# A quarter of the MLP's weight halves take their low part from an accumulating DMA

## The chip, the cores and the metric

The kernel runs on one core of a Trainium2 chip. The metric is the device time of one execution in microseconds (us), the median over runs. The kernel before took 2235.47 and 2235.57 us in its two runs, a median of 2235.52 us.

The engines are called as the profile calls them: PE (TensorE, the matrix products), PEld (its weight loads), DVE (VectorE), ACT (ScalarE), POOL (GpSimd) and SP (SyncE, which here issues the loads from HBM).

## The reference

Two layers of a decoder trunk for 256 tokens of width 2048, all float32. Each layer adds a mixing sub-layer (attention heads and state-space heads beside each other) and an MLP. Only the MLP is touched by the change:

```
D_MODEL = 2048; SEQ = 256; DEPTH = 2; D_FF = 4 * D_MODEL
h = rmsnorm(x, ln2_g)
x = x + jnp.square(jax.nn.relu(h @ w_mlp_in)) @ w_mlp_out
```

`w_mlp_in` is 2048 x 8192 and `w_mlp_out` 8192 x 2048 in each layer, 64 MB each in float32.

## The kernel before, in words

**Split products.** The products run on float32r operands. To keep the accuracy, every float32 operand is split into a high part `hi` (the value rounded to float32r) and a low part `lo` (the value minus `hi`), and a product is the sum of three: hi*hi, hi*lo and lo*hi. Activations are split once and kept; weights are split as they arrive.

**Panels, halves and steps.** All weights come in panels of 128 partitions x 2048 float32 (1 MB, one DMA on SP's queue, tile `raw`, three buffers). A step is half a panel (128 x 1024): its split and the products that it goes into. The split is one ACT copy with a cast (`hi`, line 121) and one DVE subtraction (`lo` = raw - hi, line 126). `hi` and `lo` have five buffers each (LA + 1, with LA = 4).

**Order of the program.** The kernel builds one long list of steps, 754 in all, and then writes the instructions out step by step; nothing reorders them afterwards. At step i the loop first writes the split of step i + 4 (`convert`), then the load of the panel two further on (`load_to`), then the products of step i, then, where a step ends a group, its `post`. Each engine takes its own instructions in this order and waits by semaphores. The five buffers mean that the split of step i + 4 writes the buffers that step i - 1 has read, so it starts when the products of step i - 1 are done, about when those of step i begin.

**The MLP.** It goes by eight groups of 1024 hidden columns in each layer. `mlp1` of a group has 16 steps: weights stationary (`w_units`, lines 215 to 219), eight pairs of matmuls per step, one on `hi` with 512 moving columns (activations' high and low parts side by side) and one on `lo` with 256. Every fourth step or so ends a unit of 256 hidden columns, and its post adds the two halves (ACT copy line 425, DVE lines 426 and 822) and splits the result (ACT line 121, DVE line 126 on 128 x 256). `mlp2` of a group has 16 steps too: activations stationary (`x_group`, lines 291 to 293), twelve matmuls of 512 columns per step, one third of them on `lo`; its post is two DVE instructions (line 833). The order is mlp1(0), mlp1(1), mlp2(0), mlp1(2), mlp2(1) and so on. In all there are 256 MLP steps in each layer, numbers 121 to 376 in the first and 498 to 753 in the second.

**POOL** does small elementwise work outside the MLP (and the power function of the norms, line 353); it issues no DMA before the change.

Of the kernel before, what the change touches and what calls it, by code (L numbers as in the profile page):

```python
# [31 lines left out]

# Columns of the shape-only constants.
K_ID, K_TRI, K_DIST, K_LNC, K_SEL, K_END = 0, 128, 256, 640, 1024, 1040
# Columns of the packed parameters, channels on the partitions.
V_G1, V_G2, V_GA, V_GS, V_DS, V_CW, V_CB, V_AL, V_DB, V_END = 0, 32, 64, 80, 96, 112, 208, 232, 264, 296
# [17 lines left out]
class Step:  # L54
    """Half a weight panel: its split into two float32r parts, and the products it goes into."""

    def __init__(self, panel, half, mm, post=None):
        self.panel, self.half, self.mm, self.post = panel, half, mm, post


class Panel:
    def __init__(self, src, shape):
        self.src, self.shape = src, shape
        self.raw = None
# [3 lines left out]
def trunk_kernel(ctx: ExitStack, tc, x_in, xT_in, w_in, w_v, w_dt, w_out, w1, w2, final_g, par_in, cst_in, out):  # L68
# [48 lines left out]
    def split(*parts):  # L117
        """hi + lo = src * g, each part of twelve significant bits."""
        for hi, lo, src, g in parts:
            if g is None:  # L120
                nc.scalar.copy(hi, src)  # L121
            else:
                nc.scalar.activation(hi, src, AF.Copy, scale=g)
        for hi, lo, src, g in parts:
            if g is None:
                nc.vector.tensor_tensor(lo, src, hi.bitcast(F32), op=ALU.subtract)  # L126
            else:
                nc.vector.scalar_tensor_tensor(lo, src, g, hi.bitcast(F32), op0=ALU.mult, op1=ALU.subtract)  # L128

    mm = nc.tensor.matmul  # L130

# [1 line left out]
    cst = const.tile([P, K_END], F32, name="cst")  # L133
# [51 lines left out]

# [1 line left out]
    tasks = []  # L187
# [14 lines left out]
    def stages(*fs, delay=1):  # L202
        """The first after this step or a later one, each other one a step later."""
        def g():
            for f in fs:
                f()
                yield 1
        spawn(g(), delay)

    steps = []  # L210

# [1 line left out]
    def whole_and_low(ps, wh, wl, r, k):  # L213
# [7 lines left out]
    def w_units(units, hT):  # L221
        """Weights stationary: out[col, token | its low part's products]. Two units at a time share
        the order of k so that the later half of the activations may come late."""
        def unit_steps(u):
            st = {}
            panels = [Panel(u["src"](kh), [P, 8, T]) for kh in range(2)]

            def mk(kq):
                def f(hi, lo):
                    if kq == 0:  # L230
                        st["ps"] = [acc(), acc()]
                    hv = hi.rearrange("p (k c) -> p k c", k=4)
                    lv = lo.rearrange("p (k c) -> p k c", k=4)
                    h = hT()
                    for ti in range(2):
                        ps = st["ps"][ti]
                        cs = slice(ti * P, (ti + 1) * P)
                        for kk in range(4):
                            k = kq * 4 + kk
                            r = h[k // 8][:, k % 8, :]  # L240
                            whole_and_low(ps, hv[:, kk, cs], lv[:, kk, cs], r, k)
                return f

            def post():
                for ti in range(2):
                    u["post"](ti, st["ps"][ti])

            return [Step(panels[kq // 2], kq % 2, mk(kq), post if kq == 3 else None) for kq in range(4)]

        for a in range(0, len(units), 2):  # L250
            ss = [unit_steps(u) for u in units[a:a + 2]]
            if a == 0 and len(ss) == 2:
                steps.extend(ss[0][:2] + ss[1][:2] + ss[0][2:] + ss[1][2:])
            else:
                for s in ss:
                    steps.extend(s)

    def x_group(src, nk, h_of, post, apart=False):
        """Activations stationary: out[token, 512 columns] over nk tiles of k. Apart: all of the first
        128 tokens before the second, and post by their halves."""  # L260
        st = {}
        panels = [Panel(src(i), [P, 4, 512]) for i in range(nk // 4)]

# [36 lines left out]
    def wide(w, l, r0, c0):  # L300
        """The panel of 512 rows and 512 columns from r0, c0."""
        return w[l, r0 // 512, c0 // 512]

    def tall(w, l, r0, c0):
        """The panel of 1024 rows and 256 columns from r0, c0."""
        return w[l, r0 // 1024, c0 // T]

# [1 line left out]
    def new_h():  # L309
# [5 lines left out]
    class Norm:  # L315
        """Sums of squares and split transposes of x, by its chunks of 512 columns."""

# [38 lines left out]
    def channel_rstd(ssq, n):  # L356
        """From squares with the channels on the partitions."""
        ps = sa()
        for t in range(2):
            mm(ps[:, t:t + 1], ssq[:, t * P:(t + 1) * P], ones[:, 0:1], start=True, stop=True)  # L360
        return finish_rstd(ps[:, 0:2], n)

    class FirstNorm:
        """The same from the transposed input, by its chunks of 512 channels."""

# [35 lines left out]

# [1 line left out]
    def layer(l, S, S_next):  # L403
        """S: this layer's state, with hT and norm of its first sub-layer; S_next: the next one's."""
        def rstdB_task():
# [14 lines left out]
        def joined(ps, n=P, scale=None):  # L420
            """The two halves of a weights-stationary product, summed."""
            p2 = p2p.tile([P, T], F32, tag="p2", name=nm("p2"))
# [8 lines left out]

        # x, B and C: convolution and SiLU, channels on the partitions.
        xs_t, bc_t = {}, {}
# [61 lines left out]

        # dt, the weights' two parts side by side: out[part and head, token | its low part's products].
        dts = {}
# [15 lines left out]
        steps.append(Step(Panel(w_dt[l], [P, 16, 16]), 0, dt_mm, dt_post))  # L513
        # v, tokens on the partitions.
        vt = {}
# [11 lines left out]

# [1 line left out]
        ssd = {}  # L529

        def ssd_prep():
            # dt = softplus(raw + bias), tokens on the partitions.
            ps = sa()
# [34 lines left out]
            yield 2  # L568
            # Running sums of dt * a in each chunk, and the decay to the first chunk's end.
            ps = sa()  # L570
# [48 lines left out]
        def ssd_group(g):  # L619
            """The group's inputs times dt, and its state after the first chunk."""  # L620
            xs, dt, dtd = xs_t["xs"], ssd["dt"], ssd["dtd"]
# [21 lines left out]
        def ssd_pair(j):  # L643
# [3 lines left out]
            for i in range(2):  # L647
                mm(ps[:, i * T:(i + 1) * T], sel[:, 2 * j + i:2 * j + i + 1].to_broadcast([32, P]), cumT,
                   start=True, stop=True)
            # Decays from s to t: where s is later than t, the exponent's bound keeps them finite and  # L650
            # cbs is zero.
            MT = ep.tile([P, 2, T], F32, tag="MT", name=nm("MT"))
# [47 lines left out]

# [1 line left out]
        att = {}  # L702
# [19 lines left out]
        def att_head(j, i):  # L722
            """Softmax of one head's scores; transposed, it is left in att["pt", h]."""
            q, k = att["qk", j, 0], att["qk", j, 1]
# [57 lines left out]

# [1 line left out]
        def out_post(c, which, ps):  # L784
# [28 lines left out]

# [1 line left out]
        acts = {}  # L815
# [10 lines left out]
        def mlp1(G):  # L826
            w_units([dict(src=lambda kh, u=u: tall(w1, l, kh * 1024, G * GF + u * T),
                          post=lambda ti, ps, u=u: mlp1_post(G, 2 * u + ti, ps)) for u in range(4)],
                    lambda: S["hT2"])
# [25 lines left out]
        def mlp2(G):  # L855
            for c in range(4):
                final = l == DEPTH - 1 and G == NG - 1 and c == 3
                x_group(lambda i, c=c: wide(w2, l, G * GF + i * 512, c * 512), 8,
                        lambda k: acts[G][:, k, :],
                        mlp2_last if final else lambda ps, c=c: mlp2_post(G, c, ps), apart=final)  # L860

# [6 lines left out]
    class Final:  # L868
        """The last norm and the output."""

# [46 lines left out]

# [1 line left out]
    panels = []  # L919
    for s in steps:  # L920
        if not panels or panels[-1] is not s.panel:
            if s.panel not in panels[-4:]:
                panels.append(s.panel)
    index = {id(p): i for i, p in enumerate(panels)}
    loaded = [0]

# [22 lines left out]
    def convert(s):  # L949
# [8 lines left out]
        else:  # L958
            split((s.hi, s.lo, src, None))

# [83 lines left out]
```

## Time and profile before

| | |
|---|---|
| median of two runs | 2235.52 us |
| span of the profiled execution, first to last instruction | 2233.3 us |
| PE busy | 2208.7 us, 99% of the span |
| DVE busy | 1460.3 us, 65% |
| ACT busy | 1058.4 us, 47% |
| POOL busy | 150.6 us, 7% |
| DMA engines, mean share (SP's queue) | 52.1% |

The profiled execution has its span alone on record; the runs' times lie 2.2 us above that span, which is taken as what lies around it. The row "mean share" of the DMA engines counts the time that packets took on the core's 16 DMA engines. PE's matmuls are pipelined: a matmul of 512 columns is shown with 0.39 us, but the next one starts 0.23 us after it, so the pace of PE is read from the distances between starts.

### The profile page before, as it was taken

The numbers are of one execution on the slowest core, as the hardware profiler recorded it, in microseconds if no ns is written. First come the engines' busy times: TensorE is split into PE (matmuls) and PEld (weight loads), VectorE is DVE, ScalarE is ACT, GpSimd is POOL, SyncE is SP. The second block draws the span as 40 slices with busy tenths as digits, with TensorE's granted clock in tenths as the row PEclk, the third lists the DMA queues.
The fourth block names the chain that finished last, engine by engine and source line by source line (L and its number), as shares of the span: only waits on it lengthen the run. The fifth ranks groups of instructions, "written<-read, shape, count | busy, mean of one in ns | idle before, by whom it ended". The sixth has DMA issues, their size and how long they took to land.

```text
span 2233.3 us, 29120 instructions
## 1 busy us (share of the span) xinstructions
PE 2208.7 (99%) x11444; PEld 1850.0 (83%) x11444; DVE 1460.3 (65%) x1997; ACT 1058.4 (47%) x1539; POOL 150.6 (7%) x201
## 2 busy tenths in 40 slices
PE   8999999999999999999999999999999999999998
PEld 6877778888888888888888777788888888888886
DVE  7757986665665655656666578866656656656565
ACT  6544554543444444434555455555444434444443
POOL 3102310000000000000011032100000000000001
PEclk9999999999999999999999999999999999999999
DMA  8454344555555555555554543455555555555554
GB/s 295 172 188 145 121 151 170 188 188 190 189 189 189 189 188 192 186 196 190 180 188 168 174 150 124 145 186 184 185 190 195 189 189 189 188 191 187 188 193 147
DMA packets 58249, 404.44 MB, mean 181 GB/s; under 512 B 6400, under 2 KB 6784, under 8 KB 10240
## 3 DMA queue, kind: packets, MB, share of 16 engines
q1 hardware_dynamic: 58112, 402.58, 52.1%
q8 instruction: 90, 1.47, 0.3%
q14 instruction: 47, 0.39, 0.0%
HBM read 400.45 MB, written 2.10 MB: 180 GB/s over the span
## 4 chain that ended last, share of the span: by engine, by line
PE 95%; DVE 3%; issue 1%; ACT 0%; DMA 0%; POOL 0%; SPq 0%; ACTq 0%; POOLq 0%; DVEq 0%
PE acc L215 30%; PE acc L216 15%; PE acc L291 14%; PE acc L293 14%; PE acc L292 14%; PE acc L219 2%; PE acc L218 1%; DVE lo L126 1%; PE sb L729 1%; PE sb L728 1%; DMA raw<-in_w_in 0%; PE sb L748 0%; PE sb L765 0%; PE acc L505 0%; DVE h L128 0%
## 5 line engine op out<-in xcount | busy, mean ns | idle before, releaser
L126 DVE TENSOR_TENSOR lo<-raw,hi 128x1024 fp32r<-128x1024 f32 x752 | 921.5, 1235 | 613.4 <-ACT hi L121 613.1
L121 ACT CAST hi<-raw 128x1024 fp32r<-128x1024 f32 x754 | 783.3, 1048 | 718.6 <-PE acc L293 414.2
L215 PE MATMUL acc<-h,hi 128*128 128x512 f32 x3000 | 1077.0, 401 | 8.7 <-DVE h L128 8.7
L216 PE MATMUL acc<-h,lo 128*128 128x256 f32 x3000 | 843.4, 281 | 2.2 <-DVE lo L126 2.2
L215 PEld LDWEIGHTS acc<-h,hi 128*128 128x128 f32 x3000 | 565.3, 188 | 147.1 <-issue 10.2
L216 PEld LDWEIGHTS acc<-h,lo 128*128 128x128 f32 x3000 | 568.3, 189 | 11.4 <-DVE lo L126 2.5
L291 PE MATMUL acc<-hi,m 128*128 128x512 f32 x1280 | 501.0, 391 | 0.0
L293 PE MATMUL acc<-hi,m 128*128 128x512 f32 x1280 | 498.3, 389 | 0.0
L292 PE MATMUL acc<-lo,m 128*128 128x512 f32 x1280 | 498.1, 389 | 0.0
L291 PEld LDWEIGHTS acc<-hi,m 128*128 128x128 f32 x1280 | 240.3, 188 | 51.5 <-issue 3.0
L293 PEld LDWEIGHTS acc<-hi,m 128*128 128x128 f32 x1280 | 240.3, 188 | 50.2
L292 PEld LDWEIGHTS acc<-lo,m 128*128 128x128 f32 x1280 | 240.4, 188 | 49.2
L121 ACT CAST m<-a 128x256 fp32r<-128x256 f32 x128 | 52.1, 407 | 153.6 <-DVE a L822 153.6
L425 ACT COPY p<-acc 128x256 f32<-128x256 f32 x186 | 68.9, 370 | 66.6 <-PE acc L219 61.4
L126 DVE TENSOR_TENSOR m<-a,m 128x256 fp32r<-128x256 f32 x128 | 54.4, 425 | 60.5 <-ACT m L121 60.5
L833 DVE SCALAR_TENSOR_TENSOR x_sb<-acc,r,x_sb 128x512 f32<-128x512 f32 x128 | 89.9, 743 | 4.9 <-PE acc L293 4.9
L426 DVE TENSOR_TENSOR u<-acc,p 128x256 f32<-128x256 f32 x186 | 77.2, 417 | 17.1 <-ACT p L425 17.0
L219 PE MATMUL acc<-h,hi 128*128 128x512 f32 x200 | 80.0, 400 | 0.0
L353 POOL TENSOR_TENSOR rstd<-ms,nhalf 128x2 f32<-128x2 f32 x10 | 8.8, 882 | 873.9 <-DVE ms L351 862.7
L822 DVE SCALAR_TENSOR_TENSOR a<-u 128x256 f32<-128x256 f32 x128 | 54.4, 425 | 4.4
L218 PE MATMUL acc<-h,lo 128*128 128x256 f32 x200 | 56.6, 283 | 0.0
L886 POOL TENSOR_TENSOR x_sb<-x_sb,final_g 128x512 f32<-128x512 f32 x6 | 8.6, 1454 | 687.3 <-DMA final_g<-in_final_norm_g 672.1
(167 smaller groups left out, 1169.7 us busy)
## 6 DMA issues: line engine op xcount, KB each, us to landing
raw<-in_w_mlp_in SPq DMA_DIRECT2D x128, 1024.0 KB, 4.9
raw<-in_w_mlp_out SPq DMA_DIRECT2D x128, 1024.0 KB, 4.9
raw<-in_w_in SPq DMA_DIRECT2D x69, 1024.0 KB, 4.9
raw<-in_w_out SPq DMA_DIRECT2D x32, 1024.0 KB, 4.8
raw<-in_w_v SPq DMA_DIRECT2D x16, 1024.0 KB, 4.9
raw<-in_w_in SPq DMA_DIRECT2D x6, 512.0 KB, 9.0
xT<-in_xT SPq DMA_DIRECT2D x4, 512.0 KB, 8.6
x_sb<-in_x SPq DMA_DIRECT2D x4, 512.0 KB, 6.5
```

The costliest lines, as they stand in the source:

```text
L121: nc.scalar.copy(hi, src)
L126: nc.vector.tensor_tensor(lo, src, hi.bitcast(F32), op=ALU.subtract)
L215: mm(ps, wh, r, start=(k == 0), stop=False)
L216: mm(ps[:, 0:T], wl, r[:, 0:T], start=False, stop=False)
L218: mm(ps[:, 0:T], wl, r[:, 0:T], start=False, stop=False)
L219: mm(ps, wh, r, start=False, stop=True)
L291: mm(ps, ah, hv[:, kk, :], start=(k == 0), stop=False)
L292: mm(ps, ah, lv[:, kk, :], start=False, stop=False)
L293: mm(ps, al, hv[:, kk, :], start=False, stop=(k == nk - 1))
L425: nc.scalar.copy(p2[:n], ps[:n, T:2 * T])
L426: nc.vector.tensor_tensor(u[:n], ps[:n, 0:T], p2[:n], op=ALU.add)
L833: nc.vector.scalar_tensor_tensor(xc, ps[t], S["r2"][:, t:t + 1], xc, op0=ALU.mult, op1=ALU.add)
```

## The change

Steps whose number in the list is 3 modulo 4 and whose panel belongs to the MLP (marked `far`) get `lo` in another way. ACT writes `hi` as before, then writes -hi into `lo` (the same read of `raw`, scale -1.0, rounded the same way), and then a DMA issued by POOL reads the same half panel from HBM a second time and adds it onto `lo`. There are 128 such steps, 64 in each layer. The DVE subtraction of these steps is gone. The comments that the diff also removes are not shown.

```diff
 class Panel:
-    def __init__(self, src, shape):
-        self.src, self.shape = src, shape
+    def __init__(self, src, shape, far=False):
+        self.src, self.shape, self.far = src, shape, far
...
-            panels = [Panel(u["src"](kh), [P, 8, T]) for kh in range(2)]
+            panels = [Panel(u["src"](kh), [P, 8, T], u.get("far", False)) for kh in range(2)]
...
-    def x_group(src, nk, h_of, post, apart=False):
+    def x_group(src, nk, h_of, post, apart=False, far=False):
...
-        panels = [Panel(src(i), [P, 4, 512]) for i in range(nk // 4)]
+        panels = [Panel(src(i), [P, 4, 512], far) for i in range(nk // 4)]
...
+    for i, s in enumerate(steps):
+        s.index = i
...
-            split((s.hi, s.lo, src, None))
+            far = s.panel.far
+            if far and s.index % 4 == 3:
+
+                nc.scalar.copy(s.hi, src)
+                nc.scalar.activation(s.lo, src, AF.Copy, scale=-1.0)
+                m = s.panel.shape[1] // 2
+                nc.gpsimd.dma_start(s.lo.rearrange("p (a b) -> p a b", a=m),
+                                    s.panel.src[:, s.half * m:(s.half + 1) * m, :], accum_op=ALU.add)
+            else:
+                split((s.hi, s.lo, src, None))
```

`mlp1` and `mlp2` pass `far=True` for their panels. In the changed kernel the ACT copy of such a step is line 964, the negated copy line 965 and the DMA line 967.

POOL around the start of the first layer's MLP, the kernel before (`rstd` is the power function of a norm, the second one that of the MLP's own norm):

```order
L698 TENSOR_TENSOR ssq_2353<-ssq_2353,sqy_3385 128x256 [waits Pool_49]
L353 TENSOR_TENSOR rstd_3449<-ms_3447,nhalf 128x2 [waits DVE_49]
L353 TENSOR_TENSOR rstd_3896<-ms_3894,nhalf 128x2 [waits DVE_49]
L353 TENSOR_TENSOR rstd_9571<-ms_9569,nhalf 128x2 [waits DVE_49]
L440 MEMSET ub_9742 128x4
```

POOL at the same place, the changed kernel:

```order
L353 TENSOR_TENSOR rstd_3449<-ms_3447,nhalf 128x2 [waits DVE_49]
L967 DMA lo_3811<-in_w_mlp_in 128x1024 [waits DVE_49,PE_49,Activation_49]
L353 TENSOR_TENSOR rstd_3897<-ms_3895,nhalf 128x2 [waits DVE_49]
L967 DMA lo_3922<-in_w_mlp_in 128x1024 [waits Activation_49]
L967 DMA lo_4026<-in_w_mlp_in 128x1024 [waits DVE_49,PE_49,Activation_49]
L967 DMA lo_4129<-in_w_mlp_in 128x1024 [waits DVE_49,Activation_49]
```

POOL had one instruction in the whole first MLP; now it has 64 DMAs there, and the norm's power function stands behind the first of them.

ACT in an `mlp1` of the changed kernel's first layer, from the end of one unit to the end of the next (p and m belong to the posts):

```order
L425 COPY p_1231_6537<-acc_6411 128x256
L121 CAST m_6536<-a_6541 128x256
L425 COPY p_1234_6545<-acc_6412 128x256
L121 CAST m_6536<-a_6549 128x256
L964 CAST hi_6553<-raw_6454 128x1024
L965 ACTIVATE lo_6554<-raw_6454 128x1024
L121 CAST hi_6576<-raw_6454 128x1024
L425 COPY p_1242_6596<-acc_6456 128x256
```

The negated copy of line 965 is the one new instruction on ACT in four steps. Here the whole split of the step stands behind a post, as the split of this step did before, and the next split and the next post stand behind it.

## Rows read from the trace of the kernel before

**Rows 1.** The page: span and busy time of each engine.
```profile
span 2233.3 us, 29120 instructions
PE 2208.7 (99%) x11444; PEld 1850.0 (83%) x11444; DVE 1460.3 (65%) x1997; ACT 1058.4 (47%) x1539; POOL 150.6 (7%) x201
```

**Rows 2.** Windows by stage; second and fourth are the two MLPs, with column names.
```profile
core 0: us, PE busy (x) PEld busy (x) DVE busy (x) ACT busy (x) POOL busy (x), PEclk, DMA share, GB/s
0.00:410.00 410.00, 396.93 (x2127) 324.18 (x2128) 305.33 (x480) 219.85 (x373) 75.99 (x102) 1.00 0.51 177
410.00:1115.00 705.00, 705.00 (x3581) 598.77 (x3581) 430.74 (x527) 317.09 (x411) 0.69 (x1) 1.00 0.55 189
1115.00:1510.00 395.00, 392.22 (x2128) 320.70 (x2127) 289.36 (x464) 203.87 (x348) 63.49 (x89) 1.00 0.47 161
1510.00:2215.00 705.00, 705.00 (x3572) 598.70 (x3571) 430.12 (x517) 313.00 (x401) 6.88 (x6) 1.00 0.54 188
```

**Rows 3.** PE's timeline, an mlp2 step and the next one's start (start, us).
```profile
700.85 0.39 PE L291 MATMUL acc<-hi,m 128*128 128x512 f32 x1
701.07 0.39 PE L292 MATMUL acc<-lo,m 128*128 128x512 f32 x1
701.30 0.39 PE L293 MATMUL acc<-hi,m 128*128 128x512 f32 x1
...
703.57 0.39 PE L291 MATMUL acc<-hi,m 128*128 128x512 f32 x1
703.79 0.39 PE L292 MATMUL acc<-lo,m 128*128 128x512 f32 x1
```

**Rows 4.** Timeline, an mlp1: first step's weight load, then the eleventh step's start.
```profile
719.89 0.19 PEld L216 LDWEIGHTS acc<-h,lo 128*128 128x128 f32 x1
...
748.05 0.40 PE L215 MATMUL acc<-h,hi 128*128 128x512 f32 x1
```

**Rows 5.** ACT's timeline over the same mlp1, first layer.
```profile
720.09 1.05 ACT L121 CAST hi<-raw 128x1024 fp32r<-128x1024 f32 x1 [1.67 <-PE acc L293]
...
725.61 1.05 ACT L121 CAST hi<-raw 128x1024 fp32r<-128x1024 f32 x1 [1.78 <-PE acc L215]
...
735.62 0.37 ACT L425 COPY p<-acc 128x256 f32<-128x256 f32 x1 [0.48 <-PE acc L219]
...
738.91 0.41 ACT L121 CAST m<-a 128x256 fp32r<-128x256 f32 x1 [1.01 <-DVE a L822]
739.23 2.00 ACT L121 CAST hi<-raw 128x1024 fp32r<-128x1024 f32 x2
...
745.50 2.00 ACT L121 CAST hi<-raw 128x1024 fp32r<-128x1024 f32 x2
...
756.16 2.00 ACT L121 CAST hi<-raw 128x1024 fp32r<-128x1024 f32 x2
...
767.46 2.00 ACT L121 CAST hi<-raw 128x1024 fp32r<-128x1024 f32 x2
```

**Rows 6.** Groups of DVE and ACT between 520 and 1110 us (busy, mean ns | idle before).
```profile
L126 DVE TENSOR_TENSOR lo<-raw,hi 128x1024 fp32r<-128x1024 f32 x213 | 258.8, 1224 | 209.1 <-ACT hi L121 209.1
L121 ACT CAST hi<-raw 128x1024 fp32r<-128x1024 f32 x212 | 220.6, 1051 | 258.0 <-PE acc L293 163.0 <-PE acc L215 78.1 <-issue 15.5
```

**Rows 7.** DMA issues: KB each, median us from issue to landing.
```profile
raw<-in_w_mlp_in SPq DMA_DIRECT2D x128, 1024.0 KB, 4.9
raw<-in_w_mlp_out SPq DMA_DIRECT2D x128, 1024.0 KB, 4.9
...
raw<-in_w_in SPq DMA_DIRECT2D x6, 512.0 KB, 9.0
...
cst<-in_shape_constants SPq DMA_DIRECT2D x1, 520.0 KB, 10.6
raw<-in_w_dt SPq DMA_DIRECT2D x2, 128.0 KB, 2.1
```

**Rows 8.** The page: the queue that carries the loads (packets, MB, share of 16 engines).
```profile
q1 hardware_dynamic: 58112, 402.58, 52.1%
```

**Rows 9.** SP's timeline: two loads in a row; DVE before the first.
```profile
702.13 1.22 DVE L126 TENSOR_TENSOR lo<-raw,hi 128x1024 fp32r<-128x1024 f32 x1 [1.49 <-ACT hi L121]
...
703.38 0.33 SPq L944 DMA_DIRECT2D raw<-in_w_mlp_in  x1
...
703.76 1.05 ACT L121 CAST hi<-raw 128x1024 fp32r<-128x1024 f32 x1 [1.67 <-PE acc L293]
...
708.82 0.33 SPq L944 DMA_DIRECT2D raw<-in_w_mlp_in  x1
```

**Rows 10.** POOL's smallest group, the power function on 128 x 2.
```profile
L353 POOL TENSOR_TENSOR rstd<-ms,nhalf 128x2 f32<-128x2 f32 x10 | 8.8, 882 | 873.9 <-DVE ms L351 862.7 <-DVE rd L742 11.2
```

**Rows 11.** Waits between 410 and 1115 us, longest in total first.
```profile
DVE lo L126 <- ACT hi L121: 241.1, 217, 1.7
ACT hi L121 <- PE acc L293: 171.2, 103, 1.9
ACT hi L121 <- PE acc L215: 97.0, 60, 1.8
```

More of the change, by code (lines that the diff above doesn't have):

```diff
@@ L826, in mlp1 @@
         def mlp1(G):
-            w_units([dict(src=lambda kh, u=u: tall(w1, l, kh * 1024, G * GF + u * T),
+            w_units([dict(src=lambda kh, u=u: tall(w1, l, kh * 1024, G * GF + u * T), far=True,
                           post=lambda ti, ps, u=u: mlp1_post(G, 2 * u + ti, ps)) for u in range(4)],
@@ L859, in mlp2 @@
                         lambda k: acts[G][:, k, :],
-                        mlp2_last if final else lambda ps, c=c: mlp2_post(G, c, ps), apart=final)
+                        mlp2_last if final else lambda ps, c=c: mlp2_post(G, c, ps), apart=final, far=True)
         mlp1(0)
```

## The prediction

> **What bounds the kernel now.** I read the page first: PE is busy 2208.7 of 2233.3 us, no other engine more than 65% [rows 1]. The windows by stage say where the other 25 us are: in both MLPs PE is busy 705.00 of 705.00 us at a granted clock of 1.00, and all that PE loses lies outside them [rows 2]. The change touches only the MLPs, so it enters where PE never waits. The waits of the first MLP agree: DVE waits for ACT and ACT for PE's buffers, and PE stands in no row [rows 11]. What matters is then the slack: how long before its use a step's low part is ready. It comes from three timelines. PE starts an mlp2 step at 700.85 us and the next at 703.57 us, 2.72 us each [rows 3]; in mlp1 the first step starts at 719.89 and the eleventh at 748.05 us, 2.82 us each [rows 4]. ACT splits a step four steps ahead, right when the step's buffers come free [rows 5, 9].
>
> **What is removed.** 128 DVE subtractions of 1.224 us, 157 us of DVE [rows 6]. They end far ahead of their use and DVE is busy 61% in the MLP (430.74 of 705.00) [rows 2]. PE waits for none of them, so this is worth 0 on the path.
>
> **What is added on ACT.** 128 negated copies with the shape and type of the cast next to them, 1.05 us alone and 1.00 in a row [rows 5, 6], 64 us in each MLP, where ACT is busy 317.09 of 705.00 [rows 2]. They fit into the waits for PE. Behind one stand the next split and sometimes a post; each has a step or more of slack, so 0. If ACT had no gap there, each would cost 1.0 us, 128 in all.
>
> **What is added on POOL and the DMA engines.** 128 DMAs of 512 KB. Beside them POOL has one instruction in the first MLP and six late in the second [rows 2]; the norm's power function stands behind the first DMA, which is released some three steps (8 us) before it, so 0 again.
>
> **The wait that is new.** PE's first matmul on `lo` now waits for a DMA, and PE takes its instructions in order, so everything behind it waits too. The time it is allowed (from the end of the negated copy to the use of `lo`) I call the window:
> - mlp2: the split starts at 703.76 [rows 9], two ACT instructions take 2.0, the semaphore about 0.1, so the DMA is released at 705.9. The step that uses it starts 4 x 2.72 us after 703.57, its first matmul on `lo` 0.22 later [rows 3]: 714.7. Window 8.8 us.
> - mlp1, usual: split at 725.61 [rows 5], release 727.7, use with the seventh step, 719.89 + 6 x 2.82 = 736.8 (`lo` is the weight here and loads with the step's start) [rows 4]. Window 9.1 us.
> - mlp1, late: a post stands ahead of the split on ACT. In the first layer the far steps are the 3rd, 7th, 11th and 15th of an mlp1, and the 11th is split at 739.23 instead of 736.9, behind the post that runs from 735.62 to 739.3 [rows 5]. Release 741.3, use 748.05 [rows 4]: window 6.7 us, 8 times. In the second layer, whose list starts one number later modulo 4, they are the 2nd, 6th, 10th and 14th; the 14th, and the 2nd and 6th of the stage behind, are the second of a late pair (pairs at 745.50, 756.16 and 767.46) [rows 5]. By the same working their windows are 7.9, 8.6 and 8.2 us, 8 times each.
>
> **How long the DMA takes** no row shows: nothing here is issued from POOL and nothing accumulates. From below: a plain load of 512 KB would lie between 2.1 us for 128 KB and 4.9 us for 1 MB, 3.3 us by a straight line [rows 7]. From above: the loads of this size that stood in a full queue at the kernel's start took 9.0 and 10.6 us [rows 7]; an accumulation that the engines do slowly could be longer still. I build the value from the nearest rows. It reads two streams, the half panel and `lo`, 1 MB in all, like the load with 4.9 us [rows 7]; and POOL has to make the DMA, for which I take its smallest instruction, 0.9 us [rows 10]. That is 5.8 us alone. Beside another load it shares the engines. A row of 8 KB takes 0.32 us of an engine (52.1% of 16 x 2233.3 us over 58112 packets) [rows 8], so 1 MB keeps the 16 engines for 2.6 us; sharing all of it gives 8.4 us. In the first layer the far step is the first half of its panel, and SP's loads are issued at 703.38 and 708.82, the earlier well before the accumulation's release at 705.9 [rows 9]: mostly alone, 5.8. In the second layer it is the second half, whose last reader frees the `raw` buffer that the next load waits for, so both DMAs start at one moment: 8.4.
>
> The Trainium skill ("DMA: Bandwidth & Descriptors", section "Anatomy of one DMA — SWDGE (gpsimd) path") gives about 2.0 us plus the bytes at 436 GB/s for a DMA issued from GpSimd; an estimate by that page is 4.4 us for the 1 MB of reads, no run here shows it yet, and by it the sum below would be 0 instead of 5.6 us.
>
> **The sum.** First layer: 5.8 us is inside all windows, 0. Second layer: 8 x (8.4 - 7.9) + 8 x (8.4 - 8.2) = 5.6 us. The loads of `raw` get up to 2.6 us longer; one issued at 703.38 is split two panels later, at about 714.6 [rows 3, 9], and lands by 711, so 0. The engines' share goes from 0.55 to about 0.8 (2.6 us more in each 10.9) [rows 2, 8]. Against the profiled execution: span 2233.3 + 5.6 = 2238.9, and 2.2 us lie around it, which gives **2241 us**; on the median of 2235.5 this is 0.25% more, which a measurement cannot tell from no change (the bound for that is about 2%, 45 us).
>
> **Rival 1: the DMA outlasts its window, slower.** PE's wait takes the place of nothing; it is new. Let X be the time from release to landing, in both layers. A lone late window costs X minus the window. Where every window is too short only half of that is paid: the split of the next far step is released by the step ahead of the stall, so a stall widens the next window by itself. X = 9.0 costs 8 x 2.3 + 8 x (1.1 + 0.4 + 0.8) + 56 x 0.1 = 42 us, so it decides from about 9.0 us on. X = 9.8: 25 + 38 + 56 x 0.5 + 40 x 0.35 = 105 us, 2340. X = 10.6, the slowest row [rows 7]: 31 + 57 + 56 x 0.9 + 40 x 0.75 = 168 us, **2404 us**. For it: 8.4 is close to 9.0, and the accumulation's rate is unmeasured. Against it: the engines are idle nearly half the time [rows 2], and the 9.0 and 10.6 are times behind other loads in the same queue.
>
> **Rival 2: fully hidden.** X is under 6.7 us in both layers, because the load that starts at the same moment is ahead of the accumulation or shares little with it. Then nothing is paid and the time is **2235.5 us**. It cannot be told from the forecast, and its chance goes with it.
>
> **Rival 3: POOL is held up by DVE.** POOL could be kept from making the DMA while a DVE instruction runs, 1.22 us for the longest kind there, with DVE busy 61% of the time [rows 2, 6]. X would be 7.0 and 9.6: 8 x 0.3 + 8 x (1.7 + 1.0 + 1.4) + 24 x 0.8 / 2 + 16 x 0.5 / 2 = 49 us, **2284 us**. Against it: the DVE instructions there read two operands at 1.2 ns an element, and POOL's own small ones beside DVE took 0.9 us [rows 6, 10]. The Trainium skill ("SBUF — State Buffer", section "SBUF: two separate sides") has this as a trap for DMAs issued from GpSimd beside DVE's two-port modes, and its section "Who interferes with whom" takes tensor_tensor out of it; no run here shows either.
>
> **Faster** would need time that PE loses in the MLP, and there is none [rows 2]. That the change doesn't do what it says can be left out: the order of its instructions has 128 DMAs on POOL and 128 DVE subtractions less.
>
> **Chances.** Forecast with rival 2: 0.71. Rival 1: 0.24. Rival 3: 0.04. Faster: 0.01. So faster by over 2% 0.01, within 2% 0.71, slower by over 2% 0.28. The range starts at 2231, a little under no change, and reaches to X = 9.8, 2340 us; beyond it lie about 0.16 of rival 1 and the faster case. The forecast's own range is 2233 to 2280.
>
> **What would show it.** DVE busy near 1303 us and ACT near 1190. PE busy 705 of 705 us in both MLPs if the forecast holds, with single waits under 1 us on line 216 or 292 in the second layer. The accumulating DMAs' landing time, about 6 and 8 us, and under 9 in every case. If PE's waits are at every fourth step and name the DMA, it is rival 1, and the landing time is past 9 us; if the landing is short but POOL's instruction starts late behind DVE, rival 3. The landing time is the number on which this forecast stands or falls.

## The result and the profile after

The changed kernel took 2252.6 us (2252.3 and 2252.9 in its two runs) against 2235.52 us: a ratio of 1.0076 with a 95% interval of 1.0057 to 1.0095. It is 17 us slower, three times the loss that the prediction added up, and below the 2% named there.

The page of the changed kernel: span and busy times, queues (packets, MB, share of the 16 engines), three groups, and four issues (KB each, median us to landing).

```profile
span 2250.9 us, 29606 instructions
...
PE 2210.5 (98%) x11444; PEld 1848.1 (82%) x11444; DVE 1308.1 (58%) x1869; ACT 1176.5 (52%) x1667; POOL 260.5 (12%) x329
...
q1 hardware_dynamic: 58112, 402.58, 52.0%
q0 software_dynamic: 18432, 67.12, 16.6%
...
L967 POOL DMA_DIRECT2D lo<-in_w_mlp_in x64 | 55.9, 873 | 727.0 <-ACT lo L965 660.1
L965 ACT ACTIVATE lo<-raw 128x1024 fp32r<-128x1024 f32 x128 | 134.9, 1054 | 0.0
...
raw<-in_w_mlp_in SPq DMA_DIRECT2D x128, 1024.0 KB, 5.8
raw<-in_w_mlp_out SPq DMA_DIRECT2D x128, 1024.0 KB, 5.9
...
lo<-in_w_mlp_in POOLq DMA_DIRECT2D x64, 512.0 KB, 7.9
lo<-in_w_mlp_out POOLq DMA_DIRECT2D x64, 512.0 KB, 7.2
```

Against [rows 1], DVE has lost 152 us and ACT gained 118. Against [rows 7], the loads of `raw` have become 0.9 to 1.0 us longer. A second queue, q0, keeps the DMA engines for another 16.6% of the span.

The windows of the two MLPs, columns as in [rows 2]; both are a little later and longer than there, since the work has moved:

```profile
410.00:1115.00 705.00, 704.47 (x3579) 598.51 (x3578) 353.32 (x461) 374.69 (x474) 55.52 (x64) 1.00 0.80 237
...
1520.00:2230.00 710.00, 698.07 (x3521) 589.29 (x3520) 348.69 (x448) 366.71 (x454) 60.53 (x68) 1.00 0.82 231
```

PE lost 0.5 us in the first MLP and 11.9 us in the second, where it lost nothing before. By the starts of the same instructions in both traces, the 17.6 us of longer span fall 0.5 before the first MLP, 0.8 in it, 0.9 between the two, and 15.4 from the second one's start to the end. The waits of PE in that last stretch (total, times, longest, in us):

```profile
PE acc L216 <- DMA lo<-in_w_mlp_in: 7.5, 6, 3.5
PE acc L292 <- DMA lo<-in_w_mlp_out: 2.4, 4, 1.5
PE acc L292 <- ACT lo L965: 2.0, 1, 2.0
```

These are 11 stalls and 11.9 us, the whole idle time of the window. The last row names ACT, but ACT had written that `lo` ten microseconds earlier: it is one more accumulating DMA, issued at 2201.56 us beside two 1 MB loads of SP (weights at 2201.19 and the last norm's gain at 2201.57), that took 10.5 us. A stall delays PE by some 0.2 us more than the row shows, because a matmul's shown end lies after the moment when the next could start (2017.37 to 2021.26 below, 3.89 us from start to start instead of 0.24, is shown as 3.48).

The landing times of the accumulating DMAs, first the first layer, then the second:

```profile
DMA to landing us min/median/max: 5.4/5.7/9.6
...
DMA to landing us min/median/max: 5.6/8.0/12.1
```

Both medians fit the windows of 8.8 and 9.1 us that the prediction read. The largest ones do not. The timeline around the worst stall (start, us):

```profile
2008.64 0.33 SPq L946 DMA_DIRECT2D raw<-in_w_mlp_in  x1
2009.02 0.86 POOL L967 DMA_DIRECT2D lo<-in_w_mlp_in  x1 [10.02 <-ACT lo L965]
...
2017.37 0.40 PE L215 MATMUL acc<-h,hi 128*128 128x512 f32 x1
2021.26 0.36 PE L216 MATMUL acc<-h,lo 128*128 128x256 f32 x1 [3.48 <-DMA lo<-in_w_mlp_in]
```

SP issues a load of 1 MB, and POOL issues the accumulating DMA 0.38 us behind it. PE has done the first matmul of the step, wants `lo` 8.6 us after the DMA's start, and gets it after 12.1. The DMA queues in the first 8 us after POOL's instruction, and from there to the landing (packets, MB, share of the 16 engines):

```profile
q1 hardware_dynamic: 180, 1.31, 55.6%
q0 software_dynamic: 136, 0.50, 33.8%
...
q1 hardware_dynamic: 127, 0.92, 74.0%
q0 software_dynamic: 8, 0.02, 3.0%
```

After 8 us, 136 of the 144 packets of the accumulating DMA (q0) have been started. Of the other eight, six are rows of 4 KB, and they start one after another, 0.31 to 1.15 us apart, while the next load (q1) runs. The landing waits for these few. Of the 13 landings over 8.5 us in this layer, twelve have such a tail, mostly with 0.31 us between rows, about the 0.32 us that a packet takes of one engine (16.6% of 16 x 2250.9 us over 18432 packets). So it looks like a single engine that is behind, though the records don't name the engine. The thirteenth is the one of 10.5 us, which is spread as a whole.

What a common landing in this layer looks like is seen from the DMA queues of another step whose two DMAs start in the same way (SP's at 1840.22, POOL's at 1840.60 us; landing 7.9 us). The first 4 us and the rest:

```profile
q1 hardware_dynamic: 124, 0.97, 87.6%
...
q0 software_dynamic: 144, 0.52, 69.9%
q1 hardware_dynamic: 67, 0.42, 33.7%
```

In the first 4 us the accumulating DMA moves nothing: the engines work on the load (q1) alone. All 144 packets of q0 come in the second half. So the DMA stands behind the load rather than beside it. Counted from the packet records, the first packet of such a DMA starts 1.60 us (median) after POOL's instruction in the first layer and 4.26 us after it in the second. The delay goes by the load: where it was issued 2.3, 0.8 and 0.4 us ahead of POOL's instruction, the first packet came 1.7, 3.4 and 4.3 us after that instruction, so 4.0 to 4.7 us after the load's issue each time. The middle case is in the first layer, where nine of the 64 DMAs (load 0.5 to 0.8 us ahead) landed in 7.6 to 9.6 us like those of the second.

### The profile page after: what moved, and what is told of

Read it like the earlier page. It is cut to its first block, busy times and chain, and to the rows that moved or that the text cites. A ratio compares the mean times of both kernels' runs of the same rounds, so it can differ in the third digit from the quotient of the medians.

```text
span 2250.9 us, 29606 instructions
## 1 busy us (share of the span) xinstructions
PE 2210.5 (98%) x11444; PEld 1848.1 (82%) x11444; DVE 1308.1 (58%) x1869; ACT 1176.5 (52%) x1667; POOL 260.5 (12%) x329
## 3 DMA queue, kind: packets, MB, share of 16 engines
q0 software_dynamic: 18432, 67.12, 16.6%
## 5 line engine op out<-in xcount | busy, mean ns | idle before, releaser
L126 DVE TENSOR_TENSOR lo<-raw,hi 128x1024 fp32r<-128x1024 f32 x624 | 767.3, 1236 | 759.5 <-ACT hi L121 756.6
L121 ACT CAST hi<-raw 128x1024 fp32r<-128x1024 f32 (+1 forms) x626 | 651.0, 1046 | 490.6 <-PE acc L293 269.9
L216 PE MATMUL acc<-h,lo 128*128 128x256 f32 x3000 | 844.2, 281 | 11.1 <-DMA lo<-in_w_mlp_in 8.1
L964 ACT CAST hi<-raw 128x1024 fp32r<-128x1024 f32 x128 | 134.4, 1050 | 131.5 <-PE acc L293 73.2
L967 POOL DMA_DIRECT2D lo<-in_w_mlp_in x64 | 55.9, 873 | 727.0 <-ACT lo L965 660.1
L965 ACT ACTIVATE lo<-raw 128x1024 fp32r<-128x1024 f32 x128 | 134.9, 1054 | 0.0
L967 POOL DMA_DIRECT2D lo<-in_w_mlp_out x64 | 55.7, 870 | 631.0 <-ACT lo L965 556.8
```

The source lines that it names most:

```text
L216: mm(ps[:, 0:T], wl, r[:, 0:T], start=False, stop=False)
L964: nc.scalar.copy(s.hi, src)
L965: nc.scalar.activation(s.lo, src, AF.Copy, scale=-1.0)
L967: nc.gpsimd.dma_start(s.lo.rearrange("p (a b) -> p a b", a=m), s.panel.src[:, s.half * m:(s.half + 1) * m, :], accum_op=ALU.add)
```

## The experiments

Theory A: PE waits for the accumulating DMA in the second layer because its far step is the second half of a panel, so that a load of `raw` starts at the same moment; DVE's relief and ACT's extra copies are worth nothing. Theory B: the loss comes from the busier DMA engines or from ACT, wherever the far steps lie.

**e1: far steps on the first half in both layers.** The first layer keeps its steps; in the second they move to the 1st, 5th, 9th and 13th of an `mlp1`.

```diff
-            if far and s.index % 4 == 3:
+            if far and s.half == 0 and index[id(s.panel)] % 2 == 0:
```

> The far steps are the first half of every other panel in both MLPs, 128 as before. Theory: the second layer lost time because its far step is the second half of its panel, whose negated copy frees the buffer for the next 1 MB load, so that load is issued 0.4 us ahead of the accumulating DMA and the latter's packets begin only 4.25 us after its start instead of 1.6. With the first half everywhere the second layer lands at about 5.7 us like the first, and the time is about 2238 us. Rival (the second layer loses for a reason of its own, such as its late splits or its place in the program): landing may fall, but the time stays near 2250 us.

Measured: 2239.16 us (10 runs), ratio 1.0015 (1.0006 to 1.0025). Landing times, first and second layer:

```profile
DMA to landing us min/median/max: 5.4/5.7/9.5
...
DMA to landing us min/median/max: 5.4/5.7/10.9
```

The second layer now looks like the first, and 13 of the 17 us are gone. The two waits left in it show what one late landing can do besides. PE's windows behind the longer one, a stall of 2.43 us on line 292 that ends at 2076.80:

```profile
2076.80:2080.00 3.20, 3.20 (x8) 2.52 (x9) 0.00 (x0) 0.00 (x0) 0.65 (x1) 0.50 0.88 225
2080.00:2084.00 4.00, 4.00 (x19) 3.29 (x18) 1.23 (x1) 1.20 (x2) 0.00 (x0) 1.00 0.36 72
```

The granted clock fell to 0.50, the level of 1.2 GHz, and PE is shown busy without a gap while it does 8 matmuls instead of some 14. The clock was at this level for 3.4 us, 3.2 of them behind the stall, which costs about 1.6 us more. A wait's row in the profile doesn't contain this.

**e2: far steps on the second half in both layers.** The second layer has the change's own steps; the first one's move to the 4th, 8th, 12th and 16th of an `mlp1`.

```diff
-            if far and s.index % 4 == 3:
+            if far and s.half == 1 and index[id(s.panel)] % 2 == 0:
```

> The far steps are the second half of every other panel in both MLPs, 128 as before. Theory: now the first layer collides too, lands at about 8.0 us and loses what the second lost, some 12 to 16 us more: about 2266 us. Rival (a reason of the second layer's own): no change from 2252.6 us.

Measured: 2254.48 us (2250.09 to 2259.17, 4 runs), ratio 1.0085 (1.0069 to 1.0101). Landing times by layer, and the windows of the two MLPs:

```profile
DMA to landing us min/median/max: 7.7/7.9/12.6
...
DMA to landing us min/median/max: 5.6/8.0/10.5
```

```profile
410.00:1124.00 714.00, 708.35 (x3580) 599.65 (x3579) 360.99 (x461) 374.21 (x474) 55.55 (x64) 1.00 0.84 234
1525.00:2240.00 715.00, 708.65 (x3574) 598.38 (x3574) 353.98 (x456) 370.53 (x463) 63.07 (x70) 1.00 0.82 231
```

The direction came out: the first layer now lands at 7.9 us and its MLP, which lost 0.5 us in the changed kernel, loses 5.7 us of PE's time. The size was missed, since the loss did not double: by the starts of the same instructions, the layers have 9.6 and 9.5 us too much, and the second one, with the very steps of the change, had 15.4 there. The loss consists of few outliers. A part of them belongs to the step: of the 13 landings over 8.5 us in the second layer of the changed kernel, seven come back here at the same step and within 0.3 us of the same length (8.6 to 9.1 us, and the one of 10.5), and six of its 11 stalls, 5.2 of 11.9 us, come back with them. The others, the 12.1 us among them, do not, so the loss varies from one execution to the next; the runs of this kernel lie 9 us apart.

**e3: no DMA.** DVE adds the panel onto the negated copy in the DMA's place; ACT's extra instruction stays.

```diff
-                m = s.panel.shape[1] // 2
-                nc.gpsimd.dma_start(s.lo.rearrange("p (a b) -> p a b", a=m),
-                                    s.panel.src[:, s.half * m:(s.half + 1) * m, :], accum_op=ALU.add)
+                nc.vector.tensor_tensor(s.lo, src, s.lo.bitcast(F32), op=ALU.add)
```

> The negated copy on ACT stays, but VectorE adds the panel onto it instead of the DMA. Theory: the extra 1.05 us on ACT in every fourth step costs nothing, 2236 us. Rival (the extra instruction delays the posts and the next splits on ACT and these cost the time): about 2250 us.

Measured: 2236.03 us (10 runs), ratio 1.0002 (0.9993 to 1.0012). The first MLP's window:

```profile
410.00:1115.00 705.00, 705.00 (x3583) 598.91 (x3583) 430.40 (x525) 374.78 (x474) 0.69 (x1) 1.00 0.56 190
```

ACT has the same 375 us as in the changed kernel, and PE is busy 705 of 705 us. ACT's 128 copies cost nothing; the loss belongs to the DMAs.

**e4: the same DMAs without accumulating.** They overwrite the negated copy; the addition is left out.

```diff
-                                    s.panel.src[:, s.half * m:(s.half + 1) * m, :], accum_op=ALU.add)
+                                    s.panel.src[:, s.half * m:(s.half + 1) * m, :])
```

> The same DMA from the same queue at the same place, but it overwrites lo instead of adding to it; what is left out is the addition, so lo holds the whole panel. Theory: its 4 KB rows take 0.16 us of an engine each instead of 0.33, so it lands about 1.3 us earlier, at 4.4 us in the first layer and 6.6 us in the second, and the time is 2236 to 2240 us. Rival (waiting behind the 1 MB load is all of it and the addition is free): it lands at 5.6 and 8.0 us as before, 2252 us.

Measured: 2236.81 us (10 runs), ratio 1.0006 (0.9997 to 1.0015). The queue on the page, and the landing times by layer:

```profile
q0 software_dynamic: 18432, 67.12, 8.9%
```

```profile
DMA to landing us min/median/max: 3.6/4.0/6.8
...
DMA to landing us min/median/max: 3.9/5.8/8.4
```

The same packets and bytes take 8.9% of the engines instead of 16.6%. The time is the one that my theory gave; the landings are 1.7 and 2.2 us shorter, more than the 1.3 us expected. The largest is under 8.5 us, and PE waits for none. Reading the panel a second time is harmless here; it is the accumulation's extra time that makes the slow landings too long.

**e5: twice as many accumulating DMAs.** Every first half of an MLP panel, 256 in all.

```diff
-            if far and s.index % 4 == 3:
+            if far and s.half == 0:
```

> Every first half of an MLP panel is a far step, 256 DMAs instead of 128. Theory: each accumulating row takes 0.33 us of an engine and a load's row 0.31, so a panel and its accumulation need about 5.1 us of the engines in 5.44 us of products; they nearly fill, landings spread to 6 to 9 us, and the time is 2245 to 2290 us. Rival (the DMA engines saturate, a wall of rate and not of single landings): above 2300 us. Third (the landing stays at 5.7 us): 2240 us.

Measured: 2334.08 us (4 runs), ratio 1.0427 (1.0407 to 1.0447). My theory's 2245 to 2290 was missed, and its rival held: the engines saturate. The accumulating queue on the page, the first MLP's window, and PE's waits over the whole kernel:

```profile
q0 software_dynamic: 36864, 134.23, 31.9%
```

```profile
410.00:1115.00 705.00, 673.39 (x3365) 565.43 (x3364) 258.64 (x372) 404.30 (x491) 104.54 (x120) 0.99 0.95 265
```

```profile
PE acc L216 <- DMA lo<-in_w_mlp_in: 44.2, 33, 3.3
...
PE acc L292 <- DMA lo<-in_w_mlp_out: 16.7, 19, 2.1
```

The DMA share is 0.95 (0.80 in the changed kernel), the loads take 7.3 and 7.8 us, and even the first halves land at a median of 7.9 us in the first MLP. An estimate from the pages: the loads' 0.55 of 705 us [rows 2] and q0's 31.9% of 2331.9 us, shared by two layers, are 388 and 372 us, so 760 us of the engines' time in a stage of 705. Here, and not at a quarter, the busy engines themselves are the bound. The two rows of waits are 61 of the 98 us; up to 20 more, by the working of e1, lie in 12 stretches of 3.4 us in which the granted clock was 0.50.

**e6: negate first.** The negated copy and the DMA come ahead of ACT's copy for `hi`, so the window grows by that copy's 1.05 us. The far steps are the change's.

```diff
-                nc.scalar.copy(s.hi, src)
                 nc.scalar.activation(s.lo, src, AF.Copy, scale=-1.0)
                 m = s.panel.shape[1] // 2
                 nc.gpsimd.dma_start(s.lo.rearrange("p (a b) -> p a b", a=m),
                                     s.panel.src[:, s.half * m:(s.half + 1) * m, :], accum_op=ALU.add)
+                nc.scalar.copy(s.hi, src)
```

> The far steps are those of the change, but ACT writes the negated copy before the high part, so the accumulating DMA is released one ACT instruction (1.05 us) earlier, and in the second layer now ahead of the next 1 MB load instead of 0.4 us behind it. Theory (PE waits only for landings that outlast the window, and most of the landing in the second layer is the wait behind that load): landing there 5.7 to 7 us, windows 1.05 us longer, 2236 to 2240 us. Rival (the second layer's DMAs are slow whatever stands ahead of them): landing stays at 8.0 us, the windows of 9.8 us still leave the outliers over 10 us, 2242 to 2247 us.

Measured: 2239.67 us (10 runs), ratio 1.0018 (1.0008 to 1.0027). Landing times by layer:

```profile
DMA to landing us min/median/max: 5.5/6.9/11.6
...
DMA to landing us min/median/max: 5.4/8.4/9.7
```

The time came out as my theory had it, the reason did not. The accumulating DMA is now ahead of the load, and its first packet starts 1.59 us after POOL's instruction, but it does not land earlier: the load that follows 0.56 us later shares the engines with it, so the median is 8.4 us, about what the rival had. What helped is the longer window, 9.7 and 9.9 us from POOL's start to PE's use of `lo` where the changed kernel has 8.5 and 9.0, and that no landing in the second layer took more than 9.7; two waits of 0.1 and 0.8 us are left there, both in late windows of 8.7 us. The first layer got worse: 22 of its DMAs now come 1.6 us behind a load, the median landing rose from 5.7 to 6.9 us, and the longest of 11.6 us costs a wait of 0.9 us.

**e7: e1 and e6 together.**

```diff
-            if far and s.index % 4 == 3:
+            if far and s.half == 0 and index[id(s.panel)] % 2 == 0:
...
-                nc.scalar.copy(s.hi, src)
...
+                nc.scalar.copy(s.hi, src)
```

> First half of every other panel and the negated copy ahead of the high part. Theory: landing 5.7 us against windows of 9.8 us leaves only rare outliers, 2236 to 2237 us, no faster than the kernel before, since VectorE's relief frees nothing that PE waits for. Rival (157 us less on VectorE let PE gain somewhere once the DMA is hidden): below 2230 us.

Measured: 2236.79 us (10 runs), ratio 1.0005 (0.9995 to 1.0014). Landing times by layer, and the window of the second MLP:

```profile
DMA to landing us min/median/max: 5.4/6.8/9.2
...
DMA to landing us min/median/max: 5.3/6.0/7.9
```

```profile
1520.00:2220.00 700.00, 700.00 (x3545) 594.36 (x3544) 352.98 (x452) 367.39 (x458) 63.24 (x70) 1.00 0.79 234
```

The landings are longer than the 5.7 us that my theory had, since the earlier release brings 50 of the 128 DMAs to 1.6 us behind a load. But every landing fits its window, PE is busy all the time, and the change costs nothing measurable. It gains nothing either, with 152 us less on DVE: in the MLPs PE was as full before.

**e8 and e9: more instruction fetches.** The late landings of the second layer coincide with packets of a small queue that carries instructions (q8, 90 packets of 16 KB, one about every 25 us, 0.96 us each in the median). Of its 64 accumulating DMAs in the changed kernel, 24 met such a packet between POOL's instruction and the landing, and 9 of those took over 8.5 us; of the other 40, 4 did. In e2 it is 18 of 46 against 3 of 82 in both layers. Where the packet started 4 to 7 us after POOL's instruction, while the rows of a DMA behind a load are moved, all 25 (both runs) landed at 8.3 to 9.1 us. To make it an intervention, 16 writes of a 128 x 1 tile were added to each MLP step, once with the change (e8) and once without its DMAs (e9, the control, in which DVE subtracts as before).

```diff
+    tiny = const.tile([P, 1], F32, name="tiny")
...
+            if s.panel.far:
+                for _ in range(16):
+                    nc.vector.memset(tiny, 0.0)
```

In e9 alone:

```diff
-            if far and s.index % 4 == 3:
+            if far and s.index < 0:
```

> The changed kernel with 16 tiny VectorE writes (128 x 1, to a tile that nobody reads) after each MLP step, 8192 instructions more, so that about 32 more instruction fetches of 16 KB run on the DMA engines in the two MLPs beside the 56 that are there. Theory (in the second layer PE's stalls come from accumulating DMAs that meet such a fetch, 9 of the 13 landings over 8.5 us did): more outliers in proportion, 5 to 10 us more than the change, 2257 to 2263 us. Rival (the outliers have another cause, such as HBM or the loads): 2252 us as the change.

> The control for it: the same 8192 tiny writes in a kernel without any accumulating DMA (all low parts by VectorE). Theory: loads have some 6 us of slack and VectorE's extra work is off the path, 2236 us. Rival (the tiny writes themselves cost time): as much more than 2236 as the other run is above 2252.

Measured: e8 2629.19 us (4 runs), ratio 1.1759 (1.1739 to 1.1779); e9 2758.45 us (4 runs), ratio 1.2341 (1.2323 to 1.236). The question was not answered. q8 kept its 90 packets. The other queue of this kind, q14, has more than twice as many, on the pages of the changed kernel and of e8:

```profile
q14 instruction: 49, 0.40, 0.0%
...
q14 instruction: 113, 0.93, 0.1%
```

In the second layer of e8 only 5 landings are over 8.5 us (13 in the changed kernel). But the writes were far dearer than I thought, so that the loads came at a slower pace, and the two runs can't be compared in this. The chain of waits of e9, and the group of the writes:

```profile
DVE 43%; PE 31%; issue 21%; ACT 4%; DMA 0%; DVEq 0%; POOL 0%; ACTq 0%; SPq 0%; POOLq 0%
...
L1005 DVE MEMSET tiny<- 128x1 f32 x8192 | 483.3, 59 | 503.0
```

Busy 59 ns each, with as much idle time in front, they made DVE the largest part of the chain. This shows the other side of the change: where DVE bounds, the same 128 DMAs make the kernel 129 us faster (2758.45 to 2629.19), out of the 157 us of subtractions that they replace.

## Why the prediction was right or wrong

- **What bounds the kernel: right.** PE was full in the MLP, so DVE's 152 us bought nothing (e3, e7), and they do buy time once DVE bounds (e8 against e9).
- **ACT and POOL at 0: right.** e3 has ACT's copies without the DMAs, ratio 1.0002. POOL takes 0.87 us for the instruction (0.9 estimated).
- **The windows: right.** Counted from POOL's start to the moment when PE wanted `lo`, the usual ones are 8.5 us in `mlp2` and 9.0 in `mlp1`, where 8.8 and 9.1 were read from the release, and the late ones 6.7, 7.9, 8.5 and 8.0, where 6.7, 7.9, 8.6 and 8.2 were read. e6 shows that 1.05 us more makes the difference.
- **"How long the DMA takes": failed, in its spread.** The typical values were close, 5.7 us where I had 5.8, and 8.0 where I had 8.4, the second by luck (next point). But I used one number for each layer, and said that no landing would take 9 us and no wait 1 us. In the second layer 13 of 64 landings were over 8.5 us, up to 12.1. The sum priced 16 late windows at 0.2 to 0.5 us each, 5.6 us; instead PE stalled at 11 places, 0.2 to 3.5 us each, and this stretch grew by 15.4 us. Only three of them, 1.7 of the 11.9 us, lie in the windows that I had named as late; the other eight lie in usual ones, behind landings of 8.7 to 12.1 us. In the first layer, where the median is 5.7 and the largest 9.6, one stall cost 0.5 us. That 2252.6 us is still near the forecast of 2241 is due to how few landings were that late; the sum had none of them.
- **Why it takes longer in the second layer: the place right, the mechanism wrong.** e1 and e2 show that the half of the panel decides. I had both DMAs share the engines from the start. The trace has the accumulating one idle for 4.26 us behind the load; the two ways give nearly the same landing here (8.0 and 8.4), as e6 shows, where they do share. The Trainium skill ("DMA: Bandwidth & Descriptors", section "SWDGE vs HWDGE vs iDMA") says that GpSimd's and SP's DMAs feed different queues of each engine, which serves them in turn. The trace of e6 agrees with that (from 3 to 7 us after POOL's instruction each of the two DMAs' queues started about 96 rows, in the mean over the second layer); that of the changed kernel doesn't in its first 4 us, with 124 packets of the load and none of the other. The delay goes by the load's issue (4.0 to 4.7 us behind it); whether the engines hold the packets back or the load delays the making of the DMA, no run here shows. The same page's section "Anatomy of one DMA — SWDGE (gpsimd) path" led to an estimate of 4.4 us for the 1 MB read; the measured 5.7 us differs from it.
- **The rest of the DMA terms: right.** A share of about 0.8 was forecast (0.80, 0.82 measured). The loads got 0.9 to 1.0 us longer where up to 2.6 were allowed, and PE waited for none of them.
- **Rival 1** (every window too short) did not come at a quarter. At a half (e5) 98 us are lost, but in 52 waits for 256 DMAs and with full engines, which is another mechanism. **Rival 2** (fully hidden) is the time that e7 reaches. **Rival 3** (POOL held up by DVE) fell: POOL's instruction starts 0.40 us (median) behind ACT's end and took 0.856 to 0.905 us in the second MLP. There DVE seldom ran beside it; in e8 a DVE subtraction ran beside 41 of the 128 for over 0.6 us, and these took 0.86 to 0.91 us as well. The section "Who interferes with whom" of the Trainium skill's page "SBUF — State Buffer", which takes tensor_tensor out of that trap, agrees with the trace.

Open: why single rows come so late that a landing takes 9 to 12 us. The meeting with instruction packets goes with landings of up to 9.1 us at the same steps in two runs, but it stays a coincidence in the records, as no run changed their number alone, and it doesn't account for the largest. An earlier release by a fourth `raw` buffer was not tried.

## What to carry to other kernels

A transfer fits its window only if its slow landings fit: compare the window with the largest and not with the median, above all where the release of a buffer starts a large load at the same moment. If it is tight, keep the transfer away from the large load (e1) or lengthen the window (e6); each gave back 13 of the 17 us here, and both together all of it within the noise (e7). Work taken off an engine that the bounding engine never waits for is worth nothing, and the DMA that replaces it brings a wait that was not there.

## What the runs showed of the hardware that was not expected

- Accumulating costs the DMA engines about twice the time of a plain write: by the page, 18432 packets took 16.6% of 16 x 2250.9 us, 0.32 us each, against 8.9% of 16 x 2235.2 us, 0.17 us each (e4). POOL also spends more on issuing it, 0.87 us against 0.53.
- A DMA from POOL, issued 0.4 us behind a 1 MB load from SP, moves its first packet only after 4.26 us; issued 0.56 us ahead of the load, after 1.59 us (e6). Behind the load it comes 4.0 to 4.7 us after the load's issue, whether POOL's instruction is 0.4 or 2.3 us behind it.
- A single stall of 2.4 us (e1) or 4.0 us (e2) went with a granted clock of 0.50 for 3.4 and 6.8 us. It began 0.2 and 1.8 us before the stall's end, so that 3.2 and 5.0 us of it, some 1.6 and 2.5 us of time, came on top; behind the 3.5 us stall of the changed kernel the clock stayed at 1.00.
- A late landing can be a few rows: in the one of 12.1 us, 136 of 144 packets had started after 8 us.
